# A two-layer hybrid backbone on one core: three changes of instruction order at stage borders

## The chip, the core and the metric

The program runs on one core of a Trainium2 chip. A core has a matrix engine (TensorE, PE in the profile), a vector engine (VectorE, DVE), a scalar engine (ScalarE, ACT), GpSimd (POOL) and a sync engine (SyncE, SP) that here only issues DMAs. Each works through a queue of its own; semaphores order them against each other. Matrix products land in PSUM, which has eight banks; every bank must be read out (evicted) by ACT or DVE before it can be used again. Everything else lies in SBUF or in device memory. The metric is device microseconds of one execution, the median of several.

## What is computed

Layer 0 mixes latent attention (8 heads, 2048 latent and 256 context tokens) with a bidirectional gated linear attention; layer 1 is a neighbourhood attention on a 32 by 64 grid with 16 heads. Cut to what matters here:

```python
def even_mixer(h, hc, ...):                     # layer 0
    lat = split_cols(jnp.dot(h, w_in), EVEN_SPLITS)      # latents, gates, GLA inputs
    ...
    a_x = block_attention(q_x, concat(k_x, k_c), concat(v_x, v_c), scale)
    b_x, b_c = gla_bidirectional(...)
    a = a * silu(za); b = rms_norm(b, gla_gain) * silu(zb)
    return jnp.dot(concat([a, b]), w_out)
def odd_mixer(h, hc, ...):                      # layer 1
    q_x, k_x, v_x, z_x = heads(jnp.dot(h, w_in))
    o = neighborhood_attention(q_x, k_x, v_x, k_c, v_c, rpb)   # softmax over an 8 x 16 window plus context
    return jnp.dot(o * silu(z_x), w_out)
x = x + gate * y                                # after each layer
```

## The kernel before

All data are float32. A product of two float32 matrices is made of three matrix passes: each operand is split into a high part (rounded by ACT) and a low part (the rest, by DVE), and high by high, high by low and low by high are added in one PSUM bank (`mm3`, `mm3_steps`). A weight is therefore first loaded raw (tile `wraw`, two buffers), then split in steps: SP issues the load, ACT writes the high part, DVE the low one (`split_steps`; L380 to L388). The 2304 tokens are 18 tiles of 128.

The order of each engine's queue is not the order of the program text alone. The framework plans it with a simulated timeline: an instruction that the plan finds ready may pass an earlier one that is not. `issue_after(x)` is the author's means against that: instructions of the same engine inside that block stay behind `x`. Two buffers of one name (`bufs=2`) let two uses be in flight; with one, the second use waits for the last reader of the first, a DMA out of it included.

Three places matter.

The border from `even_latent` to `even_rest` (layer 0 projections). `even_latent` runs per tile: `gemm`, then `up` one step later (queries, keys, values out of the latents), then `fin` one step after that (transposes, split into `qkhl`, stores to QT and KT). In its last two steps `first(t, j)` already makes four products of the next stage, for tiles 17 and 16 and weights 2 and 3: each fills one of two `gm` banks, is evicted by ACT into a tile named `vn`, and is stored to `Un` by a DMA on ACT's queue. The values of `up` use the same `vn`, one buffer. `even_rest` then runs products over tiles from the last to the first, with the weights in the order 2, 3, 4, 0, 1 (weight 0 lies in tiles `WU`, where w_uq lay before; weight 1 in `wr1`; weight 4 in `W2`), woven with `maxes`, score products (`mx`, L651) out of which DVE takes row maxima (L652). `maxes` loads keys (`mk`) and queries (`mq`) from KT and QT. Weights 0 and 1 are split from the list `self.ahead`, one step every fourth product step (`pump`).

The border from `even_attention` to `project` (layer 0 output). The attention loops over four head pairs `j` and five query blocks `nb`, and over 18 key tiles `n`: scores (`st`, three banks, L963 to L965), exponentials by ACT (`apt`), sums by DVE (`acc`, L954), and every fourth key tile the value products of four (`av`, L905). After the last block come the denominators (`den`, L838), two ACT operations, three of DVE, one of POOL (L847) and the store to RT. Then `project` takes tile after tile: load RT (`pr`) and the residual (`px`), split into `prh` and `prl` (`project_split`, ACT and L1055), 48 matrix passes (`pj`, four banks), gate and residual, store. Tiles 0 and 1 are loaded ahead, as the last block's loop begins; their tokens are the context, whose attention is finished much earlier. `prh` and `prl` are in a pool (`woS`) that opens when the attention's pools have closed.

`odd_vz` (layer 1 values and gates) weaves products (`gm`) with `maxes` over 16 heads: per head 16 steps `R` of two score products into `mx` banks (five of them), which DVE adds tables to and reduces (L1264, L1275). At the head's end DVE reduces once more (`mc`, L1280), PE transposes that (L1282, into an `mx` bank), ACT negates it into `mr`, and POOL issues four stores to M1 (L1286).

Of the kernel before, what the change touches and what calls it, by code (L numbers as in the profile page):

```python
# [10 lines left out]
F32 = mybir.dt.float32  # L11
F32R = mybir.dt.float32r
AF = mybir.ActivationFunctionType
# [4 lines left out]
P = 128  # L18
D = 1024
KD = D // P  # L20
# [3 lines left out]
NT = T // P  # L24
# [7 lines left out]
LAT_CHUNK = 352  # L32
# [56 lines left out]
class Kern:  # L89
# [303 lines left out]
    def even_latent(self, ws, wrest, kept):  # L393
# [5 lines left out]
        with ExitStack() as es:  # L399
# [87 lines left out]
            def up(t):  # L487
# [14 lines left out]
                vn = self.tl(sp, [P, 8, 64], "vn", bufs=1)  # L502
# [97 lines left out]
    def even_rest(self, ws, win, hT):  # L600
        nc = self.nc
        self.zaT = self.scr("zaT", (4, P, T), F32)
        with ExitStack() as es:
# [3 lines left out]
            self.ahead += [self.rest_steps(win, 0, ws, "WU"), self.rest_steps(win, 1, wp, "wr1")]  # L607
# [243 lines left out]
    def even_attention(self, ap, pp):  # L851
# [72 lines left out]
        for j in range(4):  # L924
# [12 lines left out]
            for nb, (q0, w, kts) in enumerate(blocks):  # L937
# [18 lines left out]
                for n, kt in enumerate(kts):  # L956
# [34 lines left out]
    def even_mix(self, e1, win, hT):  # L991
# [3 lines left out]
        with ExitStack() as es:  # L995
            with ExitStack() as esa:
# [5 lines left out]
                with ExitStack() as esg:  # L1002
                    gp = self.pool(esg, "glC", side="right", reuse_waits="tile")
                    gs = self.pool(esg, "glS", bufs=2, side="right", reuse_waits="tile")
                    att = self.even_attention(ap, pp)
# [195 lines left out]
    def odd_vz(self, ws, win, hT):  # L1201
# [4 lines left out]
        with ExitStack() as es:  # L1206
# [31 lines left out]

            def maxes():
                for h in range(16):  # L1240
# [11 lines left out]
                    for R in range(16):  # L1252
# [25 lines left out]
                        yield mm  # L1278
                    mc = self.tl(mp, [P, 16], "mc", bufs=1)
                    nc.vector.tensor_reduce(out=mc[:], in_=m[:], axis=AX.X, op=ALU.max)  # L1280
                    pt = self.tl(pp, [P, 512], "mx", bufs=5)
                    nc.tensor.transpose(pt[:16, :P], mc[:], self.ident[:])  # L1282
                    r = self.tl(mp, [P, P], "mr", F32R, bufs=1)
                    self.act(r[:16], pt[:16, :P], AF.Copy, scale=-1.0)
                    for g in range(4):
                        nc.gpsimd.dma_start(self.M1[h, g * 512 : g * 512 + 512].rearrange("(a c b) -> c a b", a=8, c=4),  # L1286
                                            r[4 * g : 4 * g + 4].rearrange("c (a b) -> c a b", a=8).bitcast(F32))
# [420 lines left out]
```

## Time and profile before

| | us |
|---|---|
| median of 3 runs (lowest to highest) | 3676.13 (3675.64 to 3685.73) |
| the profiled execution | 3673.37 |
| its span, first to last instruction | 3671.6 |
| PE busy in it | 3558.3 |
| DVE busy | 2360.8 |
| ACT busy | 1438.0 |
| POOL busy | 1239.9 |

Rows of a timeline give the start in microseconds from the span's start, the duration, engine, line, operation, output and inputs with their shapes, and the count of merged instructions; in square brackets stands how long the engine was idle just before, and what ended that idle time. All activations have line L106, a helper's. Rows of windows give, for a stretch of time, its length and the busy time of each engine (with the count of instructions), PE's granted clock as a share of full speed, the DMA share and GB/s.

### The profile page before, as it was taken

What the parts mean: (1) busy time and instruction counts of PE and PEld (TensorE: products, weight loads), DVE (VectorE), ACT (ScalarE), POOL (GpSimd) and SP (SyncE); (2) the same over time, 40 slices, a digit from 0 to 9 for tenths busy, and PEclk for the clock granted to TensorE, in tenths of its full rate; (3) what the DMA queues carried; (4) which work ended last, traced back from release to release, by engine and by line L of the source; (5) the groups of instructions that cost most, each with busy time, mean ns of one, the idle gap of its engine ahead of it and who ended that gap; (6) DMA issues with size and microseconds to landing.
All of it is one profiled execution on the core that took longest, in us unless ns stands there. A gap on an engine that the chain in (4) does not pass through costs nothing.

```text
span 3671.6 us, 51764 instructions
## 1 busy us (share of the span) xinstructions
PE 3558.3 (97%) x18404; PEld 2746.8 (75%) x18404; DVE 2360.8 (64%) x4846; ACT 1438.0 (39%) x2740; POOL 1239.9 (34%) x1376
## 2 busy tenths in 40 slices
PE   7999989999999999999999999999899999999899
PEld 6988988888886666655656887888788887656577
DVE  4677666888876676687765335455578784666733
ACT  5545541111115555555654114444422222555510
POOL 1434330101011121221311224333334342888863
PEclk9999999999999999999999999999999999999999
DMA  7455453222243142243623544555734446888672
GB/s 260 139 155 159 132 171 110 86 74 84 69 116 88 54 126 63 89 121 91 185 71 118 166 142 134 155 156 154 234 126 139 133 125 181 211 220 220 187 236 100
DMA packets 365780, 512.25 MB, mean 140 GB/s; under 512 B 26081, under 2 KB 245297, under 8 KB 359618
## 3 DMA queue, kind: packets, MB, share of 16 engines
q1 hardware_dynamic: 320754, 417.69, 38.7%
q0 software_dynamic: 22112, 63.26, 5.6%
q10 hardware_dynamic: 22656, 27.99, 2.2%
q8 instruction: 146, 2.39, 0.3%
q14 instruction: 112, 0.92, 0.1%
HBM read 329.45 MB, written 179.37 MB: 139 GB/s over the span
## 4 chain that ended last, share of the span: by engine, by line
PE 79%; DVE 6%; issue 5%; DMA 5%; POOL 3%; ACT 2%; SPq 0%; DVEq 0%; ACTq 0%; POOLq 0%
PE gm L129 9%; PE gm L130 9%; PE gm L131 9%; PE av L905 5%; PE mx L651 4%; PE st L963 3%; PE st L964 3%; PE st L965 3%; PE st L1361 2%; PE o L1395 2%; PE pj L129 2%; PE pj L131 2%; PE pj L130 2%; PE st L129 2%; PE st L131 2%
## 5 line engine op out<-in xcount | busy, mean ns | idle before, releaser
L954 DVE TENSOR_TENSOR acc<-acc,apt 128x512 f32<-128x512 f32 x512 | 365.6, 738 | 150.7 <-ACT apt L106 147.8
L106 ACT ACTIVATE apt<-st 128x512 f32<-128x512 f32 (+1 forms) x592 | 344.6, 594 | 281.0 <-PE st L965 245.8
L652 DVE TENSOR_REDUCE mm<-mx 128x1 f32<-128x512 f32 (+1 forms) x656 | 389.3, 629 | 82.0 <-PE mx L651 75.1
L905 PE MATMUL av<-apt,av 128*64 128x512 f32 (+1 forms) x1184 | 286.4, 597 | 0.0
L963 PE MATMUL st<-aq,akh 97*128 97x512 f32 (+1 forms) x592 | 253.0, 427 | 4.6 <-ACT apt L106 2.7
L651 PE MATMUL mx<-mk,mq 96*128 96x512 f32 (+1 forms) x656 | 236.8, 373 | 5.8 <-DMA mq<-QT 3.6
L1401 POOL TENSOR_TENSOR oacc<-oacc,opt 128x576 f32<-128x576 f32 (+5 forms) x192 | 223.8, 1191 | 39.5 <-ACT rl L106 16.6
L1519 DVE TENSOR_TENSOR opt<-st,tab 128x64 f32<-128x64 f32 (+10 forms) x576 | 144.2, 317 | 140.6 <-PE st L1362 68.1
L964 PE MATMUL st<-aq,akh 96*128 96x512 f32 (+1 forms) x592 | 233.9, 395 | 0.0
L965 PE MATMUL st<-aq,akl 96*128 96x512 f32 (+1 forms) x592 | 232.8, 394 | 0.0
L1275 DVE CUSTOM_DVE_ANT_1 mx<-mx,mtab 128x225 f32<-128x225 f32 (+13 forms) x576 | 183.7, 339 | 57.6 <-PE mx L1269 42.3
L106 ACT ACTIVATE u<-gm 128x352 f32<-128x352 f32 (+1 forms) x140 | 68.6, 498 | 371.9 <-PE gm L131 208.7
L905 PEld LDWEIGHTS av<-apt,av 128*64 128x64 f32 x1184 | 81.6, 137 | 155.5 <-issue 154.1
L963 PEld LDWEIGHTS st<-aq,akh 97*128 97x128 f32 x592 | 111.8, 189 | 97.5 <-issue 43.7
L106 ACT ACTIVATE opt<-opt 128x930 f32<-128x930 f32 (+7 forms) x129 | 104.2, 810 | 110.7 <-DVE opt L1519 102.4
L651 PEld LDWEIGHTS mx<-mk,mq 96*128 96x128 f32 x656 | 121.6, 189 | 17.3 <-issue 4.0
L965 PEld LDWEIGHTS st<-aq,akl 96*128 96x128 f32 x592 | 112.8, 191 | 25.2
L964 PEld LDWEIGHTS st<-aq,akh 96*128 96x128 f32 x592 | 113.4, 192 | 17.8
L129 PE MATMUL gm<-w1h,hhi 128*128 128x512 f32 x288 | 117.3, 407 | 7.7 <-ACT onat L106 7.7
L106 ACT ACTIVATE x<-px,modB,modA 128x128 f32<-128x128 f32 x272 | 99.3, 469 | 56.8 <-PE px L331 53.9
L129 PE MATMUL gm<-w0h,hhi 128*128 128x512 f32 x288 | 115.9, 402 | 1.9 <-DVE hhi L343 1.9
L130 PE MATMUL gm<-w1l,hhi 128*128 128x512 f32 x288 | 115.6, 401 | 0.0
(479 smaller groups left out, 9895.0 us busy)
## 6 DMA issues: line engine op xcount, KB each, us to landing
q<-Q SPq DMA_DIRECT2D x48, 512.0 KB
H<-x ACTq DMA_DIRECT2D x36, 512.0 KB
adaw<-ada_w SPq DMA_DIRECT2D x64, 256.0 KB
x<-H SPq DMA_DIRECT2D x32, 512.0 KB
wraw<-w_od SPq DMA_DIRECT2D x64, 256.0 KB
K1t<-okt POOLq DMA_DIRECT2D x32, 512.0 KB, 7.5
kt<-K1t SPq DMA_DIRECT2D x32, 512.0 KB
mtab<-rpb_q SPq DMA_DIRECT2D x16, 899.0 KB
```

Of the source, the lines that this page charges most:

```text
L106: return self.nc.scalar.activation(out, in_, func, **kw)
L129: self.nc.tensor.matmul(out, lh(k), rh(k), start=j == 0, stop=False)
L130: self.nc.tensor.matmul(out, lh(k), rl(k), start=False, stop=False)
L131: yield self.nc.tensor.matmul(out, ll(k), rh(k), start=False, stop=j == n - 1)
L651: mm = nc.tensor.matmul(ps[:, :w], q[:A_QK, (t % 6) * P : (t % 6) * P + P], k[:A_QK, k0 : k0 + w], start=True, stop=True)
L652: nc.vector.tensor_reduce(out=m[:, t, n : n + 1], in_=ps[:, :w], axis=AX.X, op=ALU.max)
L905: nc.tensor.matmul(O[j, nb][i * 64 : i * 64 + 64, :w], V[j, kt // TT][:, kt % TT, i * 64 : i * 64 + 64], pts[i][:, :w], start=n == 0, stop ...
L954: nc.vector.tensor_tensor(out=acc[i][:, :w], in0=a[:, :w], in1=pts[i][:, :w], op=ALU.add)
L963: nc.tensor.matmul(ps[:, :w], kh[: A_QK + 1, i, kq], qh[: A_QK + 1, :w], start=True, stop=False)
L964: nc.tensor.matmul(ps[:, :w], kh[:A_QK, i, kq], ql[:A_QK, :w], start=False, stop=False)
L965: mm = nc.tensor.matmul(ps[:, :w], kl[:A_QK, i, kq], qh[:A_QK, :w], start=False, stop=True)
L1401: self.psum = nc.gpsimd.tensor_tensor(out=a, in0=a, in1=pts[:, :, a0 - r0 : a1 - r0, :], op=ALU.add)
```

## The change

Three edits that do not touch the arithmetic.

First, `vn` gets two buffers, `first` remembers its latest eviction, and the split steps of weight 0 are wrapped in a new generator, `held`, by which their ACT instructions stay behind that eviction. Second, before the last attention block only tile 0 is loaded ahead, and in the middle of that block (key tile 9) its split is made, into a tile `prh` of the loading pool and into the second buffer of `px`; tile 1 is loaded in `project`. Third, in `odd_vz` the transposition of a head's maxima, its negation and its four stores move behind step R = 5 of the next head; after the last head they stand where they stood.

```diff
+    def held(self, steps):
+        while True:
+            with self.tc.issue_after(self.evicted.ins):
+                if next(steps, self) is self:
+                    return
+            yield
...
-                vn = self.tl(sp, [P, 8, 64], "vn", bufs=1)
+                vn = self.tl(sp, [P, 8, 64], "vn", bufs=2)
...
-                u = self.tl(sp, [P, LAT_CHUNK], "vn", bufs=1)
-                self.act(u[:], ps[:])
+                u = self.tl(sp, [P, LAT_CHUNK], "vn", bufs=2)
+                self.evicted = self.act(u[:], ps[:])
...
-            self.ahead += [self.rest_steps(win, 0, ws, "WU"), self.rest_steps(win, 1, wp, "wr1")]
+            self.ahead += [self.held(self.rest_steps(win, 0, ws, "WU")), self.rest_steps(win, 1, wp, "wr1")]
...
+                    if (j, nb, n) == (3, 4, NT // 2):
+                        ahead()
...
+                    pre = {}
+                    def split():
+                        r = pre[0][2]
+                        hi, lo = self.tl(ld, [P, KD, P], "prh", F32R, bufs=1), self.tl(ld, [P, KD, P], "px", F32R)
+                        self.project_split(r[:], hi[:], lo[:])
+                        pre[0] = (hi, lo, *pre[0][2:])
+                    att = self.even_attention(ap, pp, split)
...
-                        pre = {t: self.project_load(self.RT, t, self.i["xin"], ld) for t in range(2)}
+                        pre[0] = (None, None, *self.project_load(self.RT, 0, self.i["xin"], ld))
...
-            hi, lo = [self.tl(sp, [P, KD, P], "pr" + c, F32R)[:] for c in "hl"]
-            r, x = pre.pop(t) if t in pre else self.project_load(RT, t, xsrc, ld)
-            self.project_split(r[:], hi, lo)
+            if t in pre:
+                hi, lo, r, x = pre.pop(t)
+            else:
+                hi, lo = [self.tl(sp, [P, KD, P], "pr" + c, F32R)[:] for c in "hl"]
+                r, x = self.project_load(RT, t, xsrc, ld)
+                self.project_split(r[:], hi, lo)
...
+            def row(h, mc):
+                pt = self.tl(pp, [P, 512], "mx", bufs=5)
+                nc.tensor.transpose(pt[:16, :P], mc[:], self.ident[:])
+                r = self.tl(mp, [P, P], "mr", F32R, bufs=1)
+                self.act(r[:16], pt[:16, :P], AF.Copy, scale=-1.0)
+                for g in range(4):
+                    nc.gpsimd.dma_start(self.M1[h, ...], r[4 * g : 4 * g + 4]...)
...
                         yield mm
+                        if R == 5 and h:
+                            row(*turn)
                     mc = self.tl(mp, [P, 16], "mc", bufs=1)
                     nc.vector.tensor_reduce(out=mc[:], in_=m[:], axis=AX.X, op=ALU.max)
-                    pt = self.tl(pp, [P, 512], "mx", bufs=5)
-                    nc.tensor.transpose(pt[:16, :P], mc[:], self.ident[:])
...
+                    turn = (h, mc)
+                row(*turn)
```

More of the change, by code (lines that the diff above doesn't have):

```diff
@@ L849, in finish, with even_attention @@
         return rc
-    def even_attention(self, ap, pp):
+    def even_attention(self, ap, pp, ahead):
         nc = self.nc
@@ L1004, in even_mix @@
                     gs = self.pool(esg, "glS", bufs=2, side="right", reuse_waits="tile")
-                    att = self.even_attention(ap, pp)
+                    pre = {}
[5 more added lines that the diff above has]
+                    att = self.even_attention(ap, pp, split)
                     next(att)
@@ L1237, in odd_vz @@
                     nc.vector.memset(z[64 - i * 64 : 128 - i * 64].bitcast(F32), 0.0)
+            def row(h, mc):
[4 more added lines that the diff above has]
+                for g in range(4):
+                    nc.gpsimd.dma_start(self.M1[h, g * 512 : g * 512 + 512].rearrange("(a c b) -> c a b", a=8, c=4),
+                                        r[4 * g : 4 * g + 4].rearrange("c (a b) -> c a b", a=8).bitcast(F32))
             def maxes():
@@ L1278, in maxes @@
                         yield mm
+                        if R == 5 and h:
+                            row(*turn)
                     mc = self.tl(mp, [P, 16], "mc", bufs=1)
                     nc.vector.tensor_reduce(out=mc[:], in_=m[:], axis=AX.X, op=ALU.max)
-                    pt = self.tl(pp, [P, 512], "mx", bufs=5)
[L1282 to L1287, printed above, removed]
+                    turn = (h, mc)
+                row(*turn)
             cells = self.cells(list(range(NT))[::-1], (4, 5, 6, 7), lambda t, j: (j > 4 or t < NT - 2) and (j < 6 or t >= NCT))
```

## The prediction

> **What bounds the kernel now.** I read the page first: busy shares and the chain of work that ended last.
>
> ```profile
> span 3671.6 us, 51764 instructions
> ...
> PE 3558.3 (97%) x18404; PEld 2746.8 (75%) x18404; DVE 2360.8 (64%) x4846; ACT 1438.0 (39%) x2740; POOL 1239.9 (34%) x1376
> ...
> PE 79%; DVE 6%; issue 5%; DMA 5%; POOL 3%; ACT 2%; SPq 0%; DVEq 0%; ACTq 0%; POOLq 0%
> ```
>
> PE is busy 97% of the span and carries 79% of the chain. What a reorder can win at most is PE's idle time, 3671.6 - 3558.3 = 113.3 us, and stretches in which PE runs at a lower clock. So I asked next for windows around the three places.
>
> ```profile
> 515.00:558.28 43.28, 33.92 (x181) 31.91 (x181) 20.07 (x35) 16.64 (x26) 5.80 (x7) 0.84 0.55 156
> 1975.40:1990.00 14.60, 9.70 (x33) 7.41 (x32) 6.08 (x8) 5.12 (x7) 1.26 (x1) 0.77 0.63 193
> 1990.00:2190.00 200.00, 200.00 (x888) 165.15 (x887) 78.28 (x83) 36.10 (x56) 51.95 (x42) 1.00 0.51 166
> 2680.00:3080.00 400.00, 392.45 (x1931) 327.55 (x1930) 307.63 (x1292) 102.48 (x171) 167.83 (x152) 1.00 0.42 131
> ```
>
> The columns are length, then busy time of PE, weight loads, DVE, ACT and POOL, then PE's granted clock, DMA share, GB/s. Around both borders PE is idle and slow: 9.4 of 43.3 us idle at clock 0.84, and 4.9 of 14.6 us idle at 0.77, while the 200 us that follow have no idle time at all at 1.00. In the woven stage of layer 1, 2680 to 3080 us, PE lacks only 400.00 - 392.45 = 7.55 us. No other engine is near its limit in any of them (DVE is the next, 308 of 400), so a microsecond that PE does not wait there is carried to the end, as long as no later wait takes it.
>
> **First edit, border to the second half of layer 0's projections.** The timeline of PE, with one grouped row of the transposes between 515 and 560 us:
>
> ```profile
> 536.62 0.66 PE L120 MATMUL gm<-W1h,hhi 128*128 128x352 f32 x1 [5.97 <-ACT vn L106]
> ...
> 547.25 1.04 PE L549 MATMUL tp<-ident,qn 128*96 128x128 f32 x8
> ...
> 550.47 0.41 PE L129 MATMUL gm<-W2h,hhi 128*128 128x352 f32 x1
> ...
> 558.28 0.45 PE L129 MATMUL gm<-WUh,hhi 128*128 128x512 f32 x1
> ...
> 565.60 0.36 PE L651 MATMUL mx<-mk,mq 96*128 96x256 f32 x1 [3.61 <-DMA mq<-QT]
> ...
> 574.69 0.50 PE L651 MATMUL mx<-mk,mq 96*128 96x512 f32 x1 [2.16 <-DVE mm L652]
> ...
> 580.00 0.39 PE L129 MATMUL gm<-wr1h,hhi 128*128 128x512 f32 x1
> ...
> L549 PE MATMUL tp<-ident,kn 128*96 128x128 f32 x16 | 2.5, 280 | 3.2 <-DVE qkhl L553 3.2
> ```
>
> PE stands 5.97 us until an eviction frees a `gm` bank. Then two cells of 24 passes take 547.25 - 536.62 = 10.63 us, where the two cells with `W2`, of the same shape, take 558.28 - 550.47 = 7.81: 2.82 us are lost to the lower clock after the stand. Why the eviction is late is in the timelines of ACT and DVE, with two loads out of the chain:
>
> ```profile
> 524.34 2.00 ACT L106 ACTIVATE WUh<-wraw 128x1024 fp32r<-128x1024 f32 x2
> ...
> 532.95 1.06 ACT L106 ACTIVATE WUh<-wraw 128x1024 fp32r<-128x1024 f32 x1 [1.36 <-DMA wraw<-w_rest]
> ...
> 536.11 0.46 ACT L106 ACTIVATE vn<-gm 128x352 f32<-128x352 f32 x1
> ...
> 542.54 0.47 ACT L106 ACTIVATE vn<-gm 128x352 f32<-128x352 f32 x1 [5.97 <-DMA Un<-vn]
> ...
> 547.45 0.47 ACT L106 ACTIVATE vn<-gm 128x352 f32<-128x352 f32 x1 [2.07 <-PE gm L122]
> ...
> 555.82 2.01 ACT L106 ACTIVATE wr1h<-wraw 128x1024 fp32r<-128x1024 f32 x2 [0.87 <-DVE mm L642]
> ...
> 571.99 1.06 ACT L106 ACTIVATE wr1h<-wraw 128x1024 fp32r<-128x1024 f32 x1 [13.04 <-DMA wraw<-w_rest]
> ...
> 534.04 1.23 DVE L383 TENSOR_TENSOR WUl<-wraw,WUh 128x1024 fp32r<-128x1024 f32 x1 [0.25 <-ACT WUh L106]
> ...
> 574.55 1.22 DVE L383 TENSOR_TENSOR wr1l<-wraw,wr1h 128x1024 fp32r<-128x1024 f32 x1
> ...
> 527.81 5.12 DMA wraw<-w_rest
> ...
> 561.30 11.91 DMA wraw<-w_rest
> ```
>
> The first eviction (536.11) stands on ACT behind all four high splits of `WU`, the last of which waited for its raw load, and its single `vn` buffer was held by the values of `up`. The next eviction waits 5.97 us more, for the store out of that one buffer. The edit takes both reasons away: a second buffer, and `WU` behind the fourth eviction. Removed are 5.97 + 2.82 = 8.8 us. If the transposes' 3.2 us of waiting for DVE go as well, since DVE no longer has `WU`'s low parts between them, it is 12.0; I leave them in, because `qkhl` with its two buffers and stores is unchanged.
>
> Now what the moved step does where it lands. It issues four loads, four ACT and four DVE instructions, as before. From first to last these took 534.04 + 1.23 - 524.34 = 10.9 us. They may start when the fourth eviction ends, which was 547.45 + 0.47 = 547.9; the first `WU` product came at 558.28, 10.4 later, and the last of its four row pairs is used 18 passes after that, 18 x 0.225 = 4.1 us at the rate of the third window above. So `WU` fits with about 3.5 us to spare and costs nothing: the cover is the last transposes and the two `W2` cells. If one raw load takes 11.91 us, as the later one did, instead of 5.12 or less, the steps slip by some 8.5 and 5.0 of them show.
>
> `wr1` comes next, in the same two `wraw` buffers. It began at 555.82, 2.5 us before the first `WU` product; now it begins no earlier than `WU`'s end, 0.5 us after that product: 3.0 us later against PE. Its third part already waits 13.04 us for a load, and behind it on ACT stands the eviction of the first `WU` cell, behind its low part on DVE the reductions for which PE stands 2.16 us at 574.69. Low parts end at 575.8, the first `wr1` product comes at 580.00, so `wr1` itself has 4.2 us to spare, but that stand may grow by 3.0. Between 0 and 3.0 I take 3.0, since the trace of before has the very wait. The stand of 3.61 us at 565.60 (first `mq`) follows the keys' stores of the last tile, 18.35 us after its transposes began at 547.25; both move up together, so it stays. First edit: 8.8 - 3.0 = 5.8 us won, between 0.8 (with the slow load) and 12.0.
>
> The lower clock is also a rule: the Trainium skill, "TensorE: Matmul & The Clock Gate", Part 1, says that PE falls to half clock after about 3.4 us without work and rises again after about 3.4 us of work. By that page the slow stretch would cost some 1.7 us (an estimate), the first edit 1.1 less; the trace has 2.82 after one stand. It also shows a slow stretch behind two stands of 2.4 and 2.5 us, each shorter than the page's window, so the measured rows decide here.
>
> **Second edit, border to the output projection.** Rows of PE, ACT, DVE and SP:
>
> ```profile
> 1974.40 1.08 PE L838 MATMUL den<-acc,mtwos 128*64 128x512 f32 x4
> 1977.85 0.50 PE L129 MATMUL pj<-gu,prh 128*128 128x512 f32 x1 [2.37 <-ACT prh L106]
> ...
> 1981.57 0.79 PE L129 MATMUL pj<-gu,prh 128*128 128x512 f32 x1 [2.53 <-ACT prh L106]
> ...
> 1948.61 5.50 ACT L106 ACTIVATE apt<-st 128x512 f32<-128x512 f32 x8 [3.89 <-PE st L965]
> ...
> 1976.76 1.04 ACT L106 ACTIVATE prh<-pr 128x1024 fp32r<-128x1024 f32 x1
> ...
> 1980.46 1.23 DVE L1055 TENSOR_TENSOR prl<-pr,prh 128x1024 fp32r<-128x1024 f32 x1 [1.38 <-POOL rc L847]
> ...
> 1864.81 0.44 SPq L1048 DMA_DIRECT2D pr<-RT  x1
> ...
> 1947.96 32.82 SPq L848 DMA_DIRECT2D RT<-rc  x2
> ```
>
> The last denominators end at 1975.48. PE then waits 2.37 us for the high part (ACT was busy with the logarithm and exponential of the last block) and 2.53 for the low part, whose buffer waited for POOL's last product; then it is slow. From 1975.40 to 1990.00 it makes 33 passes in 14.60 us; at the rate of the next window, 200.00/888 = 0.225 us, they take 7.4. So 7.2 us go if tile 0 is ready before. Its input was issued at 1864.81 and in place by 1870 even at 5.12 us, long before key tile 9, whose exponentials are in the burst of 1948.61.
>
> The price: 1.04 us of ACT and 1.23 of DVE inside the block. ACT works 5.50 us on eight exponentials (0.69 each) and rests 3.89; in the rest the split costs 0. Inside a burst it delays PE, which has three `st` banks: 2.06 us of ACT's work less one filling and one emptying (1.38) leave 0.69, so 0.35 shows, 1.04 at most. I take 0.35. DVE rests too, and PE does not wait for `acc` before the denominators. Tile 1 loses its early place: its load is behind the RT store on SP if the plan does not lift it, and that store blocks SP until 1980.8. Then 5.12 for a load of the same 512 KB and 1.04 + 1.23 for the split make 1988.2, where tile 0's 48 passes end at 1975.5 + 10.8 = 1986.3: 1.9 us at most. Its buffer is free from the start, so I take 0. The residual of tile 1 now waits for the low part in the second `px` buffer, until 1986.3, and is needed 24 passes later (1991.7): covered, as are the weight loads queued behind it, whose layer comes 200 us on. Second edit: 6.8 us won, between 4.3 and 7.2.
>
> **Third edit, maxima of layer 1.** Waits between 2600 and 3110 us, and the tiles `mc` and `mr`:
>
> ```profile
> PE mx L1282 <- DVE mc L1280: 6.6, 10, 1.9
> ...
> ACT mz L106 <- DMA mq<-Q: 72.8, 32, 3.8
> ```
>
> ```profile
> L1280 DVE TENSOR_REDUCE mc<-mm x16: 228/236/236, 2682.9 to 3066.1; 128x16 f32<-128x80 f32 x16
> ...
> L1286 POOL DMA_DIRECT2D M<-mr x64: 568/582/657, 2684.1 to 3073.2; - x64
> L106 ACT ACTIVATE mr<-mx x24: 250/267/269, 652.7 to 3070.8; 16x128 fp32r<-16x128 f32 x16, 18x128 fp32r<-18x128 f32 x8
> ```
>
> PE waits 6.6 us in ten places, up to 1.9, for the last reduction of a head. Six steps later that reduction is long done. Fifteen of sixteen heads move: 6.6 x 15/16 = 6.2 us. The step takes along one transposition, one ACT instruction and four POOL issues of 0.58 us; their number does not change. POOL, busy 168 of 400 us, has 2.3 us of issues per head later in its queue, with table additions and V stores around them; nothing on PE waits for POOL in this stage. No wait of PE for an `mx` bank is among the waits, so I take 6.2; the most is the stage's whole idle time, 7.5.
>
> **The sum.** 5.8 + 6.8 + 6.2 = 18.8 us. Against the profiled execution, 3673.37 (span 3671.6 and 1.8 around it), that is 3654.6. The median of the runs stands 2.8 above that execution, so the forecast for a median is 3676.13 - 18.8 = 3657.3.
>
> **Rivals.** (a) The first edit gives nothing: the plan puts the second eviction behind `up`'s values in the second buffer, or `WU`'s load is slow, and the stand only moves to the first `WU` product. For it: the 11.91 us load and the 13.04 us wait behind it. Against: 3.5 us of spare. Won 6.8 + 6.2 = 13.0: 3663. (b) The stands come back elsewhere in two of the three places, because the planner lays the queues anew from the first changed instruction on; what is left is about one term, 6.5: 3669.6, no change that can be told. Against it: PE had no idle time at all in the 200 us behind the second place.
>
> (c) Slower. The transposition now sits in the middle of a head, where ACT's queue also holds the `mz` copies that wait for `mq`, 32 times, up to 3.8 us. If `mr` stands behind one, its `mx` bank stays taken for 3.8 + 0.3 = 4.1 us. A head lasts (3066.1 - 2682.9)/15 = 25.5 us and uses 24 banks, 1.06 us each; four banks carry 4.2 us, less the 1.9 by which DVE lags, 2.3. PE then stands 1.8 us a head, 15 times, 27 us, and the third edit's gain is gone: + 27 - 12.6 = 14 slower, 3690. It decides from 0.84 us a head, where it eats the other two gains. Against it: the same copies stand around the head border now, and no wait for a bank is seen.
>
> **How the numbers follow.** Forecast 0.53, (a) 0.17, (b) 0.18, (c) 0.12. A measurement of this kernel tells 0.3%, 11 us, from no change. Forecast and nearly all of (a) are faster by more: 0.68; (b) and the rest of (a) are the same: 0.20; slower 0.12. The bounds of the terms give gains of 12.0 + 7.2 + 7.5 = 26.7 (3649.4) down to 0.8 + 4.3 + 0 = 5.1 (3671.0); I widen by the 2.8 that runs differ from the profile, to 3646 and, toward (c), to 3677.
>
> **What would show it.** In the profile after: the four evictions of `first` ahead of every `WU` split on ACT, no wait of PE on `vn` over 1 us, PE's clock above 0.9 between border and first `W2` cell; `pj` within 0.5 us of the denominators; no row of L1282 waiting for `mc` but the last head's. Wrong would be: PE waiting for `WU` low parts or longer than 5 us at 574.69's place, `st` rows waiting for ACT over 1 us near key tile 9, or waits of L1262 and L1269 for banks behind `mr`.

## The result, and the profile after

The changed kernel takes 3654.62 us (median of 5 runs, 3651.06 to 3663.0), the kernel before 3677.92 beside it (5 runs, 3675.64 to 3685.73). The ratio is 0.9937, with a 95% interval of 0.9925 to 0.9949: 23.3 us faster, 18.8 forecast. The profiled execution took 3652.31 us. The page of the changed kernel:

```profile
span 3650.5 us, 51811 instructions
...
PE 3552.0 (97%) x18404; PEld 2747.6 (75%) x18404; DVE 2355.2 (65%) x4846; ACT 1433.2 (39%) x2740; POOL 1234.9 (34%) x1376
...
PE 5%; DMA 0%; DVE 0%; POOL 0%; ACT 0%; issue 0%; DVEq 0%; ACTq 0%; SPq 0%; POOLq 0%
```

The span is 21.1 us shorter. PE's busy time fell by 6.3 us for the same 18404 passes, so part of the gain is clock and not idle time. The chain of waits covers only the span's last 5% in this profile, and says nothing of the three places; so I compare windows. In the code after, lines are shifted by 8 to 32 (L549 is now L557, L651 L659, L963 L972, L1262 L1294); the transposition of L1282 has moved up to L1264.

Windows of the kernel before: four between the last pass of `up` and the first `wr1` product (cut at the first `W2` product, the first `WU` product and the first `mx` product), the attention from the first score to the last denominators, from there to the 49th `pj` pass, and the woven stage of layer 1 from its first to its last maximum. Columns as in the prediction.

```profile
526.98:550.47 23.49, 14.29 (x75) 12.96 (x73) 13.12 (x23) 8.79 (x15) 4.90 (x5) 0.78 0.66 200
550.47:558.28 7.81, 7.81 (x52) 7.74 (x49) 3.07 (x6) 3.73 (x5) 0.00 (x0) 1.00 0.75 187
558.28:565.60 7.32, 3.71 (x17) 2.71 (x16) 0.99 (x1) 0.47 (x1) 1.35 (x2) 1.00 0.93 260
565.60:580.00 14.40, 12.24 (x48) 9.60 (x49) 6.92 (x12) 3.23 (x5) 0.09 (x1) 0.88 0.46 135
...
1099.95:1974.89 874.94, 866.44 (x4228) 535.40 (x4227) 608.51 (x878) 482.15 (x955) 175.24 (x168) 0.99 0.32 94
1974.89:1994.07 19.18, 14.28 (x52) 10.79 (x49) 7.21 (x10) 5.85 (x9) 2.55 (x2) 0.82 0.67 205
2653.06:3064.41 411.35, 403.80 (x1997) 337.63 (x1996) 327.55 (x1348) 110.35 (x182) 171.88 (x145) 1.00 0.40 126
```

The same seven windows of the kernel after:

```profile
526.48:541.67 15.19, 11.42 (x74) 10.94 (x73) 10.30 (x20) 6.87 (x12) 5.17 (x5) 0.90 0.76 207
541.67:553.68 12.01, 9.73 (x50) 9.44 (x48) 5.65 (x8) 5.83 (x8) 0.00 (x0) 0.84 0.84 253
553.68:560.85 7.17, 3.75 (x15) 2.76 (x16) 0.86 (x1) 0.30 (x1) 1.35 (x2) 1.00 0.93 252
560.85:573.08 12.23, 10.43 (x47) 7.86 (x47) 5.45 (x9) 3.20 (x4) 0.00 (x0) 1.00 0.52 161
...
1093.58:1973.60 880.02, 868.01 (x4228) 537.96 (x4227) 607.59 (x879) 479.92 (x956) 170.25 (x168) 0.99 0.33 93
1973.60:1985.18 11.58, 11.58 (x52) 9.12 (x49) 4.53 (x5) 3.25 (x4) 1.29 (x1) 1.00 0.43 138
2640.96:3044.75 403.79, 401.98 (x1994) 337.29 (x1995) 324.41 (x1347) 110.34 (x183) 174.40 (x146) 1.00 0.41 131
```

Length less PE's busy time is idle time; busy time for the same passes falls as the clock rises. The first place shrinks in its first window by 8.30 us, gives back 4.20 in the second, and wins 0.15 and 2.17 in the others; of these 6.42 us, 5.88 are left at the last maximum of layer 0. The second place falls to 11.58 us: 52 passes, no idle time, full clock. The third falls by 7.56. The attention, which only the second edit touches, is 5.08 us longer.

The first place in the timeline of PE after:

```profile
540.11 1.91 PE L557 MATMUL tp<-ident,kn 128*96 128x128 f32 x8 [3.77 <-DVE qkhl L561]
...
553.68 0.50 PE L129 MATMUL gm<-WUh,hhi 128*128 128x512 f32 x1 [2.28 <-ACT u L106]
...
560.85 0.36 PE L659 MATMUL mx<-mk,mq 96*128 96x256 f32 x1 [3.42 <-DMA mq<-QT]
...
569.67 0.38 PE L659 MATMUL mx<-mk,mq 96*128 96x256 f32 x1 [1.61 <-DVE mm L660]
```

The timeline of ACT there:

```profile
525.99 0.47 ACT L106 ACTIVATE vn<-gm 128x352 f32<-128x352 f32 x1
...
535.51 0.46 ACT L106 ACTIVATE vn<-gm 128x352 f32<-128x352 f32 x1 [3.37 <-PE gm L122]
535.87 1.05 ACT L106 ACTIVATE WUh<-wraw 128x1024 fp32r<-128x1024 f32 x1
...
536.81 1.05 ACT L106 ACTIVATE WUh<-wraw 128x1024 fp32r<-128x1024 f32 x1
537.76 1.25 ACT L106 ACTIVATE qkhl<-tp,qkg 96x512 fp32r<-96x512 f32 x2
...
552.22 1.06 ACT L106 ACTIVATE wr1h<-wraw 128x1024 fp32r<-128x1024 f32 x1 [2.40 <-DMA wraw<-w_rest]
553.18 0.80 ACT L106 ACTIVATE u<-gm 128x352 f32<-128x352 f32 x2
...
566.97 1.06 ACT L106 ACTIVATE wr1h<-wraw 128x1024 fp32r<-128x1024 f32 x1 [12.98 <-DMA wraw<-w_rest]
```

And of DVE:

```profile
536.95 2.36 DVE L391 TENSOR_TENSOR WUl<-wraw,WUh 128x1024 fp32r<-128x1024 f32 x2 [3.21 <-ACT WUh L106]
539.22 1.40 DVE L561 SCALAR_TENSOR_TENSOR qkhl<-tp,qkg,qkhl 96x512 fp32r<-96x512 f32 x2
```

The evictions into `vn` (first 525.99, fourth 535.51) now stand ahead of all `WU` splits, and no pass waits for `vn`. But the first two splits went in front of the last tile's `qkhl` on both engines (535.87 and 536.81 before 537.76; 536.95 before 539.22), and the transposes stand 3.77 us for it. (In the kernel before, `qkhl` followed the eviction at once, at 547.89, and the same transposes waited 1.21 us.) A second stand, 2.28 us at the first `WU` product, is new: the eviction (553.18) is queued on ACT behind the second `wr1` split, which waited 2.40 us for its raw load. The stands for `mq` (3.42) and for a reduction (1.61) remained, the latter still beside the third `wr1` split's wait of 12.98 us for its load (13.04 before).

The second place: PE, then ACT and SP some 85 us earlier.

```profile
1973.11 1.08 PE L846 MATMUL den<-acc,mtwos 128*64 128x512 f32 x4
1974.12 0.50 PE L129 MATMUL pj<-gu,prh 128*128 128x512 f32 x1
```

```profile
1881.58 0.51 SPq L1068 DMA_DIRECT2D pr<-RT  x1
...
1887.86 1.06 ACT L106 ACTIVATE prh<-pr 128x1024 fp32r<-128x1024 f32 x1 [3.74 <-DMA pr<-RT]
...
1889.46 0.50 PE L972 MATMUL st<-aq,akh 97*128 97x512 f32 x1 [0.67 <-ACT apt L106]
```

`pj` follows the denominators without a gap. The split was written at key tile 9 of the last block, but the plan set it some 60 us ahead, in the block before (1887.86), where ACT waited 3.74 us for its load. PE waited 0.67 us for the exponentials behind it; value products and scores covered the rest.

PE's waits between 2620 and 3110 us in the third place:

```profile
PE tp L1251 <- DVE ovz L1248: 1.0, 1, 1.0
PE mx L1301 <- DVE mm L1307: 0.6, 1, 0.6
PE mx L1294 <- ACT mz L106: 0.6, 1, 0.6
```

No wait for `mc` is left. Last, what PE waits for within the attention, before and after (total, times, longest):

```profile
PE st L963 <- ACT apt L106: 2.7, 2, 1.4
PE st L963 <- DMA aq<-QT: 1.2, 1, 1.2
```

```profile
PE st L972 <- DMA aq<-QT: 4.4, 2, 2.3
PE st L972 <- ACT apt L106: 4.4, 3, 2.3
```

The waits for queries (`aq`) grew from 1.2 to 4.4 us and those for exponentials from 2.7 to 4.4. No term of the prediction stands for this. The longest wait for queries is at the first wide block of the second head pair:

```profile
1322.65 0.47 PE L972 MATMUL st<-aq,akh 97*128 97x512 f32 x1 [2.33 <-DMA aq<-QT]
```

SyncE issues that load at 1314.23, once the block two before has ended, and PE then has work until 1320.32. In the kernel before, the load went out at 1324.48, and the plan left PE work up to the scores that need it (1332.61), so nothing waited.

### The profile page after: what moved, and what is told of

The parts are those of the page before. It is cut to its first block, busy times and chain, and to the rows that moved or that the text cites. A ratio compares the mean times of both kernels' runs of the same rounds, so it can differ in the third digit from the quotient of the medians.

```text
span 3650.5 us, 51811 instructions
## 1 busy us (share of the span) xinstructions
PE 3552.0 (97%) x18404; PEld 2747.6 (75%) x18404; DVE 2355.2 (65%) x4846; ACT 1433.2 (39%) x2740; POOL 1234.9 (34%) x1376
## 5 line engine op out<-in xcount | busy, mean ns | idle before, releaser
L963 DVE TENSOR_TENSOR acc<-acc,apt 128x512 f32<-128x512 f32 x512 | 375.6, 756 | 168.5 <-ACT apt L106 165.6
L972 PE MATMUL st<-aq,akh 97*128 97x512 f32 (+1 forms) x592 | 256.6, 434 | 8.8 <-DMA aq<-QT 4.4
L659 PE MATMUL mx<-mk,mq 96*128 96x512 f32 (+1 forms) x656 | 235.8, 373 | 5.0 <-DMA mq<-QT 3.4
L1307 DVE CUSTOM_DVE_ANT_1 mx<-mx,mtab 128x217 f32<-128x217 f32 (+12 forms) x576 | 184.2, 338 | 40.1 <-PE mx L1301 30.9
L972 PEld LDWEIGHTS st<-aq,akh 97*128 97x128 f32 x592 | 113.0, 191 | 99.1 <-issue 50.5
L659 PEld LDWEIGHTS mx<-mk,mq 96*128 96x128 f32 x656 | 121.2, 188 | 16.8 <-DMA mk<-KT 3.8
L807 POOL TENSOR_TENSOR gsf<-gsf,D 64x512 f32<-64x512 f32 x17 | 25.1, 1477 | 271.4 <-DVE D L784 271.4
```

Of the source, the lines that this page charges most:

```text
L659: mm = nc.tensor.matmul(ps[:, :w], q[:A_QK, (t % 6) * P : (t % 6) * P + P], k[:A_QK, k0 : k0 + w], start=True, stop=True)
L963: nc.vector.tensor_tensor(out=acc[i][:, :w], in0=a[:, :w], in1=pts[i][:, :w], op=ALU.add)
L972: nc.tensor.matmul(ps[:, :w], kh[: A_QK + 1, i, kq], qh[: A_QK + 1, :w], start=True, stop=False)
L1307: nc.vector.tensor_tensor_reduce(out=s, in0=s, in1=tb[:, ri : ri + rn, ci : ci + cn], scale=1.0, scalar=-3e38, op0=ALU.add, op1=ALU.max, a ...
```

## The experiments

All lengths below are of PE in each kernel's profiled execution: "layer 0 projections" from the last pass of `up` to the last maximum of layer 0, "attention", "output border" and "layer 1 maxima" as in the windows above.

| kernel | layer 0 projections | attention | output border | layer 1 maxima |
|---|---|---|---|---|
| before | 562.50 | 874.94 | 19.18 | 411.35 |
| after | 556.62 | 880.02 | 11.58 | 403.79 |
| first edit only | 556.75 | 881.45 | 18.74 | 411.56 |
| second only | 562.38 | 878.84 | 11.58 | 412.74 |
| third only | 562.66 | 877.30 | 18.17 | 408.70 |
| buffers of the first only | 559.19 | 880.61 | 19.71 | 411.41 |
| hold of the first only | 557.01 | 876.34 | 19.48 | 411.90 |
| all, split held | 556.70 | 880.36 | 11.58 | 403.30 |
| all, `wr1` held | 554.95 | 882.34 | 11.58 | 403.71 |
| all, step 0 | 556.24 | 881.03 | 11.58 | 404.69 |
| first edit, context queries apart | 555.83 | 870.30 | 16.08 | 411.64 |
| before, context queries apart | 562.42 | 872.90 | 16.11 | 411.45 |
| all, context queries apart | 556.78 | 873.26 | 11.58 | 403.76 |
| the same, `wr1` held | 557.10 | 873.03 | 11.58 | 401.51 |

**One edit at a time.** Each of three kernels keeps one edit of the change and undoes the two others.

First edit only, second and third undone (the lines that set them to work):

```diff
-                    if (j, nb, n) == (3, 4, NT // 2):
-                        ahead()
...
-                        if R == 5 and h:
-                            row(*turn)
```

> First edit alone. After all three edits the end of layer 0's woven stage came 6.4 us earlier, but the attention behind it took 5.1 us more (880.0 against 874.9 us from first score to last denominators). Theory 1 (each edit acts at its own place, the attention's loss belongs to the second edit, whose load and split lie in it): 6.4 us earlier at the end of the woven stage, attention 874.9 +- 0.7, span 3671.6 - 6.4 = 3665.2. Rival (the planner lays the attention anew because of the first edit): the same 6.4, attention about 880, span about 3670.

Second edit only:

```diff
-            self.ahead += [self.held(self.rest_steps(win, 0, ws, "WU")), self.rest_steps(win, 1, wp, "wr1")]
+            self.ahead += [self.rest_steps(win, 0, ws, "WU"), self.rest_steps(win, 1, wp, "wr1")]
...
-                u = self.tl(sp, [P, LAT_CHUNK], "vn", bufs=2)
+                u = self.tl(sp, [P, LAT_CHUNK], "vn", bufs=1)
...
-                        if R == 5 and h:
-                            row(*turn)
```

> Second edit alone. Both theories: first output product right behind the last denominators, 7 to 7.6 us won there. Theory 1: attention about 879 to 880 us because of the second edit, span 3671.6 - 7.5 + 5 = 3669. Rival: attention 875 to 875.6 (only the 0.67 us for which scores waited behind the split that itself waited 3.74 us for its load), span 3671.6 - 7.5 + 0.7 = 3664.8.

Third edit only:

```diff
-            self.ahead += [self.held(self.rest_steps(win, 0, ws, "WU")), self.rest_steps(win, 1, wp, "wr1")]
+            self.ahead += [self.rest_steps(win, 0, ws, "WU"), self.rest_steps(win, 1, wp, "wr1")]
...
-                    if (j, nb, n) == (3, 4, NT // 2):
-                        ahead()
```

> Third edit alone. Theory: the 6.6 us of waits for the head's last reduction go but for the last head, 6 to 7.2 us earlier at the end of layer 1's woven stage and at the end, span about 3665; everything before 2650 us as before, to 0.5 us. Rival (the 7.1 us came from the layers' changed phase and not from the edit): under 3 us, span above 3668.5.

Measured: 3665.41 us (10 runs; ratio 0.9974, 0.9963 to 0.9985), 3668.76 (10; 0.9979, 0.9970 to 0.9989) and 3669.34 (10; 0.9975, 0.9964 to 0.9986), against 3676.35 before (25 runs). The product of the three ratios is 0.9928, beside 0.9937 (0.9925 to 0.9949) for all: the gains add up within the noise.

The table puts two of the gains where they belong: 5.75 us in the layer 0 projections with the first edit, 7.60 at the output border with the second (always to 11.58). The attention is longest with the first edit (881.45), which changes no line of the attention. The second alone has 878.84, between both expectations and close to the one that blamed the second edit, so one profile of this stage does not decide; I come back to it below. The third alone wins only 2.65 in its stage, less than the 6 expected. Its profile is that of the slowest of its ten runs (3677.69 us), and its last `up` pass comes 3.6 us later than before the change, though no edit acts ahead of that pass. The `mc` waits are gone there too, but PE's waits between 2620 and 3120 us show another in their place:

```profile
PE tp L1246 <- DVE ovz L1243: 5.0, 1, 5.0
```

It is one wait of 5.0 us for a copy of DVE, which ends 10 us into the stage. The full change waits 1.0 us at that line. The six other profiles with this edit have 1.2 us or less there, and 401.51 to 404.69 us for the stage, so the 5.0 us belong to this one profile or its plan; no run tells which.

**The two halves of the first edit.** One kernel has the second `vn` buffer without the hold, the other the hold with one buffer; neither has the second and third edit.

The buffers, starting from the first edit alone:

```diff
-            self.ahead += [self.held(self.rest_steps(win, 0, ws, "WU")), self.rest_steps(win, 1, wp, "wr1")]
+            self.ahead += [self.rest_steps(win, 0, ws, "WU"), self.rest_steps(win, 1, wp, "wr1")]
```

> Of the first edit only the second vn buffer; weight 0's splits are free to pass the evictions again. Stretch from the last pass of up to the last maximum of layer 0: 562.4 to 562.7 us in the three kernels without the first edit, 556.6 to 556.8 with it. Theory (two causes, the buffer and the place behind the four splits, each holds the eviction by itself): under half of the 5.8 us, 560 us or more. Rival (the buffer is the whole cause): 556.7.

The hold, starting from the first edit alone:

```diff
-                vn = self.tl(sp, [P, 8, 64], "vn", bufs=2)
+                vn = self.tl(sp, [P, 8, 64], "vn", bufs=1)
...
-                u = self.tl(sp, [P, LAT_CHUNK], "vn", bufs=2)
+                u = self.tl(sp, [P, LAT_CHUNK], "vn", bufs=1)
```

> Of the first edit only the hold: splits of weight 0 behind the fourth eviction, with one vn buffer. Theory: evictions wait in turn for up's store and for each other's store out of the one buffer, about 2.5 us after up's values and then some 6 us each, so PE still stands and the splits come later still: 562 us or more for the stretch, 566 if the splits show in full. Rival (the hold is the whole cause): 556.7.

One run each: 3670.72 and 3669.62 us. PE's waits from 526 to 585 us, first with the buffers, then with the hold:

```profile
PE tp L557 <- DVE qkhl L561: 4.0, 3, 2.5
PE mx L659 <- DVE mm L660: 3.5, 1, 3.5
PE mx L659 <- DMA mq<-QT: 2.0, 1, 2.0
PE gm L120 <- ACT vn L106: 1.9, 1, 1.9
```

```profile
PE gm L129 <- ACT u L106: 6.1, 1, 6.1
PE gm L120 <- ACT vn L106: 4.3, 1, 4.3
```

My theory that each half holds its own share of the stand falls. The buffers alone win 3.31 of 5.88 us, the hold alone 5.49, though it keeps 4.3 us of waiting for `vn` and adds 6.1 at the first `WU` product. While PE stands there, loads, splits and reductions get done, and the later waits for `mq` and `mm` are gone. Between the last `up` pass and the first `wr1` product PE is idle 14.97 us before, 11.38 with the buffers, 10.37 with the hold, 11.26 after: stands at this border move more than they vanish. The second buffer adds 0.39 us to the hold, by one profile of each.

**Is the split in the attention the cause of its loss?** All three edits, with the early split held behind the exponential of its key tile, so that the plan can't lift it:

```diff
-                        self.act(pt[:, :w], ps[:, :w], AF.Exp, scale=A_SCALE)
+                        ex = self.act(pt[:, :w], ps[:, :w], AF.Exp, scale=A_SCALE)
...
-                        ahead()
+                        with self.tc.issue_after(ex.ins):
+                            ahead()
```

> All three edits, and the split of output tile 0 kept behind the exponentials of key tile 9, where the text puts it; the plan had lifted it 60 us ahead, where ACT waited 3.74 us for its load. Theory: what that wait costs PE is the 0.67 us that scores waited, span 0.5 to 1 us below that of all three edits (3650.5). Rival (that wait is behind the attention's loss of 5.1 us): attention back to 875, span about 3646.

3656.9 us (4 runs; ratio 0.9950, 0.9931 to 0.9969), the attention at 880.36, 0.34 off. The rival falls: ACT's 3.74 us in front of the split are not the loss. The 0.5 to 1 us that I expected did not come either. The split now stands at 1949.25 and PE waits for nothing there, but at the old place it still waits 0.63 us for exponentials (at 1893.04), so even the 0.67 us can't be put down to the split.

**Where the transposition stands.** Step 0 of the next head instead of step 5:

```diff
-                        if R == 5 and h:
+                        if R == 0 and h:
```

> All three edits with the transposition behind step 0 of the next head instead of step 5. A step takes 25.5/16 = 1.6 us, the longest wait was 1.9. Theory (only DVE's lag at the head's end matters): waits for mc under 1 us in sum, stage 403.5 to 405 us, the same as step 5. Rival (the bank behind the transposition and what DVE still owes need more distance): waits of 2 us or more, stage 406 or more.

3658.19 us in one run, the stage at 404.69, waits for `mc` 0.94 us in all. One step takes nearly all of the gain; steps 1 to 5 are worth at most some 0.9 us, by one profile.

**The wait at the first `WU` product.** `wr1`'s splits are held behind the evictions of the two `W2` cells:

```diff
-    def held(self, steps):
+    def held(self, steps, behind=None):
...
-            with self.tc.issue_after(self.evicted.ins):
+            with self.tc.issue_after((behind() if behind else self.evicted).ins):
...
-            self.ahead += [self.held(self.rest_steps(win, 0, ws, "WU")), self.rest_steps(win, 1, wp, "wr1")]
+            self.ahead += [self.held(self.rest_steps(win, 0, ws, "WU")), self.held(self.rest_steps(win, 1, wp, "wr1"), lambda: self.drained)]
...
-                    self.act(u[:, :w], ps[:, :w])
+                    e = self.act(u[:, :w], ps[:, :w])
+                    if t >= NT - 2:
+                        self.drained = e
```

> All three edits, and weight 1's splits kept behind the evictions of the two weight 4 products, which stood behind one of them for a raw load (PE waited 2.28 us). Theory: that wait goes, first product of weight 0 about 2 us earlier, but weight 1's later loads slip by as much, so the stretch from the last pass of up to the last maximum gets 0 to 2 us shorter than 556.6. Rival (the held splits of weight 1 come too late for their products): longer than 558.

3658.23 us in one run; the stand of 2.28 is gone, the stage 1.67 shorter, but the next stand, for `mq`, grew from 3.42 to 5.08. Beside the query change below, the same hold won nothing (557.10 against 556.78).

**The queries.** The first query block of each head pair, the context, is 256 wide and short, the four others are 512 wide; all use `aq` with two buffers, so a block's queries can be loaded only when the block two before it has ended. The edit gives the context's queries a buffer of their own, so that the load behind a context block need not wait. First beside the first edit alone, then beside none:

```diff
-            q = self.tl(ap, [P, 4, 512], "aq", F32R, bufs=2)
+            q = self.tl(ap, [P, 4, 512], "aq", F32R, bufs=2) if w > CTX else self.tl(ap, [P, 4, CTX], "aqc", F32R, bufs=1)
```

> First edit alone, with a query buffer of its own for the context block of each head pair, so that the next block's queries load one block earlier. With the first edit the attention waits 5.4, 4.4 and 5.6 us for queries (1.2 to 2.9 without it) and takes 880 to 881.5 us instead of 875 to 879. Theory (the attention's loss is this wait, in a plan that the first edit shifted): waits for queries under 1 us, attention 876 or less, span 5 us below the first edit alone (3664.5). Rival (the loss is in other waits or in the clock): attention still 879 or more.

> The kernel before with the context query buffer and none of the three edits. Theory (the attention's loss with the first edit is the wait for queries, so without that wait both plans of the attention cost the same): attention 869 to 872, as in e7, no waits for queries, span about 3668. Rival (the plan that the first edit makes is itself the shorter one once queries are there): 873 or more.

Beside the first edit: 3658.82 us (4 runs; ratio 0.9943, 0.9927 to 0.9960), attention 870.30 instead of 881.45. Beside none: 3667.72 (10 runs; 0.9974, 0.9962 to 0.9985), attention 872.90, a little over what was expected. No wait for queries is left in either. So the first edit's loss in the attention lies in the waits for queries as the plan spreads them: with these gone, the attention with the first edit (870.30, 873.26, 873.03) is as short as without (872.90). One stand tells the plans apart: that of 2.33 us at 1322.65, shown above, is in all five profiles with the whole first edit and the original queries (2.33 to 3.05 us) and in none of the five without the whole edit.

**All edits with the query buffer.** So that it fits, the high part of tile 0 uses the second `pr` buffer:

```diff
-                        hi, lo = self.tl(ld, [P, KD, P], "prh", F32R, bufs=1), self.tl(ld, [P, KD, P], "px", F32R)
+                        hi, lo = self.tl(ld, [P, KD, P], "pr", F32R), self.tl(ld, [P, KD, P], "px", F32R)
```

> All three edits with the context query buffer, whose place is made by writing tile 0's high part into the second pr buffer in place of a new tile. With the first edit alone that buffer took the attention from 881.5 to 870.3 us. Theory (terms add): attention about 870, first stretch 556.6, output projection 11.6 from denominators to its 49th pass, layer 1's woven stage 403.8, span about 3641, 0.25% below all three edits. Rival (the shared pr buffer delays tile 1's load, or the attention falls back to waiting): over 14 us in the projection's start, or attention above 876, span above 3648.

3646.83 us (6 runs, 3643.92 to 3650.86), against 3678.14 before (17 runs): ratio 0.9914, 0.9901 to 0.9928. It beats the kernel before. Its slowest run is faster than the fastest of the kernel after (3651.06), beside which it was not run; the intervals of the two ratios just overlap, so that it beats that one too is likely and not shown. The span is 3645.4 us where 3641 was expected; 3.3 us of that are the attention (873.26 for 870). PE's waits within its attention:

```profile
PE st L972 <- ACT apt L106: 5.8, 4, 2.0
PE gl L822 <- ACT gsb L106: 1.4, 1, 1.4
```

With the hold of `wr1` added:

> The same and weight 1's splits held as in e8, which shortened the first stretch from 556.6 to 555.0. Theory: first stretch 555, all else as e9, span 1 to 2 us below e9's, which runs cannot tell from it. Rival (a new plan of the attention): attention above 874, span above e9's.

3648.35 us (ratio 0.9915, 0.9902 to 0.9929), the same. The layer 0 projections stayed at 557.10 instead of the 555 hoped for. The one long stand left there:

```profile
563.49 0.55 PE L661 MATMUL mx<-mk,mq 96*128 96x256 f32 x1 [6.41 <-DMA mq<-QT]
```

It is the same stand for `mq`, now 6.41 us. What is won ahead of it is waited for at it. SyncE's rows show why: it issues the loads of keys and queries only when the last tile's keys have been stored. It waited 2.0 us for that store before the change (then `mq` went out at 558.60), 4.3 after it (553.77) and 4.6 here (555.91); a raw weight load is now issued just ahead of that store, and whether this slows the store was not tested. In the eight profiles with the whole first edit the first `mx` product comes 33.5 to 35.0 us after the last `up` pass, whatever stands before it, and 38.6 in the kernel before.

## Why the prediction was right

The forecast was 3657.3 us, within 3646 to 3677 and faster by more than 0.3%; measured are 3654.62 and 0.63% (0.51 to 0.75). The three places and their causes were right; that the sum is so close is in part luck, as the last terms of the table show. Term by term against the profiled executions:

| term | predicted | measured |
|---|---|---|
| first edit, layer 0 projections | 5.8 | 5.88 |
| second edit, output border | 7.2 | 7.60 |
| second edit, price in the attention | -0.35 | -0.67 |
| third edit, layer 1 maxima | 6.2 | 7.56 |
| attention, other than that price | 0 | -4.4 |
| stages that no edit touches | 0 | 5.1 |
| sum | 18.8 | 21.1 |

The loss of 4.4 us in the attention and the 5.1 us of stages that no edit touches nearly cancel; neither was forecast.

**First edit: the sum held, its parts did not.** "Removed are 5.97 + 2.82 = 8.8" was right: the first window lost 8.30, with 0.54 more of waiting for `qkhl` in it. "`WU` fits with about 3.5 us to spare and costs nothing: the cover is the last transposes and the two `W2` cells" is the step that failed. It counted the time of the cover, and not who feeds it: the transposes wait for `qkhl`, made by the same ACT and DVE that now do the splits. The transposes' waits, which I had left in at 3.2, came as one stand of 3.77, and it drew a slow stretch: the two `W2` cells took 9.73 us of PE time, 7.81 before. My mark "PE's clock above 0.9 between border and first `W2` cell" is met only just (0.905), since most of that slow stretch falls into the next window (0.84). That the splits in front of `qkhl` make the stand is read from the rows of ACT and DVE; no run puts them behind it.

"That stand may grow by 3.0" had the right cause at the wrong place: ACT's evictions were late behind a `wr1` split that waited for its load, but 16 us earlier, at the first `WU` product (2.28 us); the stand for the reduction shrank from 2.16 to 1.61. The fourth window then won 2.17, of which 1.81 are busy time, since this time no slow stretch followed the stand for `mq`. With the first edit alone the same border shows no such luck: a longer stand for `mq` (5.0 us), a clock of 0.79 in the fourth window, and yet 556.75 for the stage. So that 5.8 was met by 5.88 is luck in its parts: a stand priced at nothing and a stretch of full clock that nobody counted. In the lower bound, the slip of 8.5 us is not the difference of the two loads given for it (11.91 - 5.12 = 6.8); by that, 3.3 us and not 5.0 would show.

**Second edit: right.** 2.37 + 2.53 us of stands and the slow stretch behind them are gone, tile 1 cost nothing (no idle time in 11.58 us). The price was not the guessed half of a burst's delay: the plan moved the split ahead until its input was late, and with the split at its written place PE waited for nothing there. The 0.67 of the table is the wait behind the split and, by that run, not surely its doing.

**Third edit: right, mis-sized.** The 6.2 counted idle time alone. Idle time fell by 5.74 (7.55 to 1.81), and PE's busy time by 1.82, at a clock of 1.00 in both. The rows do not show longer passes behind the stands: the transposition takes 0.27 us after a stand (at 2683.26) as without one (2759.28), and the score pass behind it 0.36 in both cases. Summed from each pass's start to the next one's, 1.1 us of the 1.82 lie in the score passes of 256 columns and 0.4 in the transpositions, which now stand at another place among the passes, and two to three passes fewer lie in the window. Why they are cheaper there was not tested. Rival (c) needed `mr` behind the `mz` copies to hold a bank: PE waits for no `mr`; a `mz` copy ends one wait of 0.6 us, for an operand, and one of 0.2 us.

**What was missing.** That an edit in one stage replans another was my rival (b), at two of three places and 0.18. It happened once in the full kernel, in the attention, 550 us behind the edit. With the original queries the attention takes 874.9 to 880.6 us in the five profiles without the whole first edit (877.6 in the mean) and 880.0 to 882.3 in the five with it (881.0): a loss of about 3 us, 5.1 between the two profiles compared. The stand for queries at 1322.65 costs 2.33 us and then the clock: the 6.82 us from 1323.84 on have a clock of 0.50 and PE busy throughout, 3.4 us lost. Other stands and slow stretches of the attention differ too; in all, 3.51 of the 5.08 us are idle time and 1.57 busy time.

**What stays open.** 5.1 us of the 21.1 lie in stages that no edit touches (3.2 in the preparation of layer 1's queries and keys, 1.8 in its attention). Over the 14 profiles the same two stages differ by 5.7 us (451.3 to 457.0) and 5.5 (566.7 to 572.2), so one pair of profiles can't assign them. For the same reason the first edit's 10.9 us by medians (3676.35 to 3665.41) is not found in its two stages, which give 5.75 less about 3; the rest was not located.

## What to carry to other kernels

A split, load or copy that is hidden under PE's work is hidden only as far as its engines do not also feed that work: list what ACT and DVE owe the cover before calling it free. Where several waits follow each other at a border, count the idle time of the border as a whole, since removing one stand lengthens the next until the last load in the row sets the end. After an edit that a planner sees, compare the lengths of all stages, and look there for buffers too few; here one buffer for the short query block was worth about as much as an edit.

## What the runs showed of the hardware

A short stand costs PE its clock. In the 14 profiles PE stands 2.2 us or longer in 161 places (after its first 60 us), and in the 5 us that follow, the granted clock is between 0.50 and 0.77 in 159 of them, 0.59 in the mean. The two others, at 1.00, are the stands of 2.28 and 3.42 us in the kernel after. Of the 50 stands between 1.8 and 2.2 us, 19 are followed by full clock; one stand of 1.87 us, at the same pass of the same stage in every profile, by 1.00 in nine and by 0.66 in five.

The records of the granted clock show what lies behind this scatter. In each profile the clock changes only on a raster of 3.41 us. Behind the first 60 us there are 221 stretches of half clock, and 87, 105, 24 and 5 of them last one, two, three and four steps. Whether one begins goes with how long PE was busy in the step before it: of the steps at full clock, those with PE busy below 45% were followed by half clock in 141 of 142 cases, those from 45 to 75% in 77 of 250, those above in 3 of 13970. Steps of the kernel after: the one in which the stand of 3.77 us begins, the slow stretch behind it, and four around the stands of 2.28 and 3.42 us:

```profile
535.36:538.77 3.41, 0.98 (x9) 0.73 (x7) 1.82 (x2) 3.26 (x5) 0.00 (x0) 1.00 0.19 67
538.77:545.60 6.83, 5.49 (x21) 5.45 (x22) 3.08 (x4) 2.04 (x3) 0.00 (x0) 0.50 0.93 265
...
549.01:552.43 3.42, 2.39 (x15) 2.10 (x14) 1.22 (x1) 1.02 (x2) 0.00 (x0) 1.00 1.00 303
552.43:555.84 3.41, 2.16 (x9) 1.80 (x10) 1.23 (x1) 1.55 (x3) 1.35 (x2) 1.00 0.61 155
555.84:559.26 3.42, 1.59 (x7) 0.94 (x5) 0.00 (x0) 0.00 (x0) 0.00 (x0) 1.00 0.98 240
559.26:562.67 3.41, 1.82 (x9) 1.58 (x10) 0.42 (x1) 0.00 (x0) 0.00 (x0) 1.00 1.08 357
```

The first step has 0.98 us of work, and two slow steps follow. The two later stands are each cut by an edge of the raster, so that no step has less than 1.59 us of work (47%), and the clock stays. So where a stand falls on the raster decides, which no edit here controls. A slow stretch costs half of PE's busy time in it: 1.7 us for one step, 2.8 for two, 2.4 in the mean of the 221 (worked out from these records).

The Trainium skill, "TensorE: Matmul & The Clock Gate", Part 1, puts the loss of the clock at an idle window of about 3.4 us, and says that this window runs freely and does not start anew with a kernel. The raster of 3.41 us and the scatter at 1.87 us agree with the free window. That a whole window must be idle does not agree: 98 of the 161 stands are shorter than 3.41 us, and 97 of these were followed by a slow stretch. The prediction's estimate by that page (1.1 us less for the first edit) was not borne out: PE's busy time in the first window fell by 2.87 us, and the rows had said 2.82.
